# Turning the first two row tiles of a decoder block before their norm factor is known, and applying 1/rms to three half banks and to h later

## The chip, the cores and the metric

One core of a Trainium2 chip runs the whole kernel, float32 in and out. The metric is the device time of one execution in microseconds (us). Seven engines or queues matter: TensorE (PE, with PEld for its weight loads), VectorE (DVE), ScalarE (ACT), GpSimd (POOL) and the DMA queue that SyncE (SP) feeds.

## What is computed

A hybrid decoder block of 512 tokens and 1024 channels. The change touches only its first step, the RMS norm of the input and the first columns of the input projection:

```python
h = rmsnorm(x, norm1_g[l])            # x * 1/rms(token) * g(channel)
z = h @ w_in[l] + b_in[l]             # 1024 -> 6656 columns
z_glu, z_rx, z_rg, z_ga, z_gb = jnp.split(z, split_idx, axis=-1)
u = z_glu[..., :D_CONV] * jax.nn.sigmoid(z_glu[..., D_CONV:])
...
xb = causal_depthwise_conv(z_rx, lru_conv_w[l], lru_conv_b[l])
hb = rg_lru(xb, lru_wa[l], lru_ba[l], lru_wx[l], lru_bx[l], lru_lambda[l])
...
x = x + m @ w_mix_out[l]
h = rmsnorm(x, norm2_g[l])
x = x + (jax.nn.silu(h @ ffn_w1[l]) * (h @ ffn_w3[l])) @ ffn_w2[l]
return rmsnorm(x, norm_f_g)
```

Since 1/rms depends on the token alone, `(x * r) @ w` is also `(x @ w) * r`, token by token.

## The kernel before

**Split products.** Each factor of a product is held as two parts, a high part h (a cast to the fp32r type) and a low part l (the rest, `full - h`). A product is three matmuls per 128 channels: high weight by high input, high by low, low by high (`mm3`). An input projection tile is 128 output columns by 512 tokens, eight channel tiles c = 0 to 7, so 24 matmuls of 512 tokens, or twice 24 of 256 tokens when the two halves of the tokens are done apart.

**Weights** come as chunks of 512 KB, in a fixed list: SP loads a chunk into a raw buffer, ACT casts its high part (`L123`), POOL or DVE subtracts for the low part (`L119`). The first chunk (`in0`, columns 0 to 127) comes in two halves and goes through `first_parts` (L131): DVE casts the first half (`L133`), POOL casts the second and subtracts both. The second chunk (`in8`, columns 1024 to 1151, the gate of the same pair) is cast by ACT in two halves (`L138`, `L139`) and its low part is DVE's.

**The start** is the first block with a hand-written order on all engines (from L707). The four row tiles x0 to x3 hold 128 tokens each, with tokens on the partitions. For x0 and x1, DVE sums the squares of the second half of the channels (`half_sum`, L656), ACT those of the first half and then takes the root (`root`, L661 and L662), DVE takes the reciprocal, and DVE or ACT multiply the tile by it (`scale_half`, L672 and L670). Only then PE turns the tile, eight 128 by 128 transposes of it (`turn_rows`, L635), into banks tx of PSUM, 256 tokens of x0 and x1 next to each other. From these banks ACT writes the high part of the normed and weighted input for each channel tile (h10h to h17h, `turned_parts`, L644) and DVE the low part (h10l to h17l, L645). The name h13h is read as: first norm, channel tile 3, high part. Before any of that PE runs `WARM` matmuls on a tile of ones (L543).

PE then works through the half tiles in this order: `in0` for the first 256 tokens (`early_first`, L689, 24 matmuls in a hand-made order), `in8` for the first 256 (`early_mm(1, 0)`, L573), the turning of x2 and x3, `in1` for the first 256, `in0`, then the turning of the parameter rows (`L552`), `in8` and `in1` for the second 256, and `in9` for all 512 (`early_whole`). The banks are called z, with the column tile's number. x2 and x3 take the same road as x0 and x1 (half sum, root, reciprocal, scaling, turning), from data that are loaded behind the first two weight chunks.

**After that** a second hand-ordered block runs the other projection tiles, in which DVE's convolution steps are placed beside PE's tiles by a planner with fixed costs. `glu` joins banks z0 and z8 (a bias on ACT, a tanh on ACT, `u` on DVE at L915).

Of the kernel before, what the change touches and what calls it, by code (L numbers as in the profile page):

```python
# [33 lines left out]
HL = 5  # L34
AHEAD = 4
BEHIND = 5
WARM = 13

PACK = HB // 2
ROWS_G = HB + PACK  # L40
# [45 lines left out]
def tile_block(ctx, tc, a, out):  # L86
# [31 lines left out]
    def sub(eng, o, x, y):  # L118
        return eng.tensor_tensor(out=o, in0=x, in1=y, op=ALU.subtract)  # L119

    def split_to(h, l, full, eng, copy=act.copy):
# [6 lines left out]
        newest["sub" if eng is pool_e else "low"] = last.ins  # L128
        return h, l

    def first_parts(h, l, full):  # L131
        for cs in (slice(0, T), slice(T, 2 * T)):
            (pool_e if cs.start else vec).tensor_copy(h[:, cs], full[:, cs])  # L133
            newest["sub"] = sub(pool_e, l[:, cs], full[:, cs], h[:, cs].bitcast(F32)).ins
        return h, l

    def copy_halves(h, full):
        act.copy(h[:, :T], full[:, :T])  # L138
        act.copy(h[:, T:], full[:, T:])  # L139

    def lows_put_off(behind):
        while put_off:
# [55 lines left out]
    def emit_to(n):  # L198
        while emitted[0] < min(len(chunks), n):
            emit_chunk()  # L200
# [433 lines left out]
            at += P * (t % 2)  # L634
            pe.transpose(ps[b][:, at : at + P], xt[t][c // 4][:, (c % 4) * P : (c % 4 + 1) * P], ident)  # L635

    def turned_parts(hf, ps, some=range(ND)):
        cs = slice(hf * 256, hf * 256 + 256)
        for c in some:
            g = pc("norm1_g", c)  # L640
            b, at = spot(c, ps)
            p_ = ps[b][:, at : at + 256]
            h, l = (v[:, cs] for v in h1p[c])
            act.activation(h, p_, AF.Copy, scale=g)  # L644
            vec.scalar_tensor_tensor(out=l, in0=p_, scalar=g, in1=h.bitcast(F32), op0=ALU.mult, op1=ALU.subtract)  # L645

    def parts_of(pair_tiles, cs=slice(0, T)):
        return [(h[:, cs], l[:, cs]) for h, l in pair_tiles]
# [16 lines left out]
    def first_sums(t):  # L665
        return root(t, half_sum(t))
# [9 lines left out]
    EARLY_IN = [(GLU + j + 8 * o) for j in range(EARLY) for o in range(2)]  # L676
    early = []

    def early_first(between):
        m = EARLY_IN[0]  # L680
        early.append((m, w_tiles(f"in{m}", ND, 0), bank(f"z{m}")))
        _, ws, ps = early[0]
        order = [(0, 0), (0, 1), (1, 0), (0, 2), (1, 1), (0, 3), (1, 2), (2, 0), (2, 1), (2, 2), (0, 4), (2, 3), (1, 3), (0, 5)]
        order += [(1, 4), (0, 6), (1, 5), (2, 4), (0, 7), (2, 5), (2, 6), (1, 6), (2, 7), (1, 7)]
        xs = parts_of(h1p, HALVES[0])
        for n, (m, c) in enumerate(order):
            (wh, wl), (xh, xl) = ws[c], xs[c]
            l, r = ((wh, xh), (wh, xl), (wl, xh))[m]
            pe.matmul(ps[:, HALVES[0]], l, r, start=n == 0, stop=n == len(order) - 1)  # L689
            if n == 0:  # L690
                between()

    def early_mm(i, hf):
        m = EARLY_IN[i]
        if hf == 0:
            early.append((m, w_tiles(f"in{m}", ND, 0), bank(f"z{m}")))
        _, ws, ps = early[i]
        mm3(ps[:, HALVES[hf]], ws, parts_of(h1p, HALVES[hf]), lo_last=hf == 0)

    def early_whole(i):  # L700
        m = EARLY_IN[i]
# [5 lines left out]
    with tc.manual_schedule(engines={ET.PE, ET.Activation, ET.DVE, ET.SP, ET.Pool}):  # L707

        turned = [(bank if q < 5 else bank2)(f"tx0{q}") for q in range(6)]
        r0 = first_sums(0)  # L710
        vec.reciprocal(r0, r0)
        r1 = first_sums(1)
        scale_half(0, 0, r0)
        turn_rows(0, turned, 0)
        scale_half(0, 1, r0, True)
        rows_turned(0, n_first)
        vec.reciprocal(r1, r1)
        scale_half(1, 0, r1)
        turn_rows(1, turned, 0)
        emit_to(1)  # L720
        scale_half(1, 1, r1)
        turn_rows(0, turned, 1)
        load_chunk(1)
        load_x(2)
        load_x(3)
        load_chunk(2)
        load_chunk(3)
        turned_parts(0, turned, range(4))
        early_first(lambda: (turn_rows(1, turned, 1), turned_parts(0, turned, range(4, ND))))
        r2 = half_sum(2)  # L730
        emit_to(2)
        root(2, r2)
        early_mm(1, 0)
        vec.reciprocal(r2[1], r2[1])
        junk = [shortt(f"n1j3{h}") for h in range(2)]
        r3 = rstd_begin(xt[3][0], junk[0])
        for h in range(2):
            scale_half(2, h, r2[1])
        turned = [(bank2, bank)[q // 2](f"tx1{q}") for q in range(4)]
        turn_rows(2, turned)  # L740
        r3 = rstd_end(r3, xt[3][1], junk[1])
        for h in range(2):
            scale_half(3, h, r3)
        emit_to(3)
        load_head_rows()
        for i in range(len(parts)):
            if i not in first:
                load_rows(i)
        turn_rows(3, turned)
        emit_to(4)  # L750
        turned_parts(1, turned)
        early_mm(2, 0)
        early_mm(0, 1)
        rows_turned(n_first, n_rows)
        for m, n in ((GLU, 16), (GB, 8)):
            cols = par[:, col["b_in"] + m : col["b_in"] + m + n]
            act.activation(cols, cols, AF.Copy, scale=0.5)
        for i in (1, 2):
            early_mm(i, 1)
        early_whole(3)  # L760
    h1 = parts_of(h1p)

# [941 lines left out]
```

## Time and profile before

| what | value |
|---|---|
| three runs | 788.32, 788.86, 788.87 us; median 788.86 |
| the profiled execution's own time | 787.63 us |
| its span, first to last instruction | 785.9 us |
| PE busy | 777.6 us, 99% of the span |
| DVE, ACT, POOL busy | 86%, 60%, 46% |
| first projection matmul starts | 8.85 us into the span |
| `in9` starts (end of the start block's half tiles) | 29.34 us |

The page's chain that ended last follows work back from the last instruction: here it is PE nearly throughout. A row of the timeline gives the start, the duration, the engine, the line, the operation, what is written from what, and in brackets how long the engine had been idle and what released it. Durations overlap from one row to the next on the same engine, since an instruction begins before the one ahead of it has drained; the pitch from start to start is what a queue of them costs.

### The profile page before, as it was taken

The numbers are of one execution on the slowest core, as the hardware profiler recorded it, in microseconds if no ns is written. First come the engines' busy times: TensorE is split into PE (matmuls) and PEld (weight loads), VectorE is DVE, ScalarE is ACT, GpSimd is POOL, SyncE is SP. The second block draws the span as 40 slices with busy tenths as digits, with TensorE's granted clock in tenths as the row PEclk, the third lists the DMA queues.
The fourth block names the chain that finished last, engine by engine and source line by source line (L and its number), as shares of the span: only waits on it lengthen the run. The fifth ranks groups of instructions, "written<-read, shape, count | busy, mean of one in ns | idle before, by whom it ended". The sixth has DMA issues, their size and how long they took to land.

```text
span 785.9 us, 12508 instructions
## 1 busy us (share of the span) xinstructions
PE 777.6 (99%) x4328; PEld 680.0 (87%) x4328; DVE 677.2 (86%) x1074; ACT 473.8 (60%) x696; POOL 363.2 (46%) x353
## 2 busy tenths in 40 slices
PE   8999999999999999999999999999999999999996
PEld 8988888888888888888888898999999999888885
DVE  6389998889887987999799869897887897999956
ACT  7543678966785686564235676445545455656844
POOL 3367876799788989754530380121322322000000
PEclk9999999999999999999999999999999999999999
DMA  7656989899989868998978675688999998778652
GB/s 225 180 150 183 280 229 275 244 277 265 253 244 311 259 199 251 309 296 260 323 258 293 189 214 182 205 281 288 366 318 325 311 344 294 248 233 269 219 171 108
DMA packets 188561, 199.04 MB, mean 253 GB/s; under 512 B 15290, under 2 KB 149586, under 8 KB 188498
## 3 DMA queue, kind: packets, MB, share of 16 engines
q1 hardware_dynamic: 178066, 161.80, 68.2%
q0 software_dynamic: 10272, 36.18, 13.4%
q8 instruction: 34, 0.56, 0.3%
q14 instruction: 29, 0.24, 0.1%
q10 hardware_dynamic: 160, 0.27, 0.1%
HBM read 146.30 MB, written 38.80 MB: 236 GB/s over the span
## 4 chain that ended last, share of the span: by engine, by line
PE 99%; DVE 0%; issue 0%; ACT 0%
PE z L573 36%; PE fr L1429 25%; PE or L1195 13%; PE yb L573 7%; PE ya L573 6%; PE mxr L1195 5%; PE f L573 3%; PE g L1021 2%; PE fr L1475 1%; PE warm L543 1%; PE tx L635 0%; PE th L618 0%; PE z L689 0%; ACT of L1645 0%; PE orl L1195 0%
## 5 line engine op out<-in xcount | busy, mean ns | idle before, releaser
L821 DVE SCALAR_TENSOR_TENSOR cv<-u,par,cv 128x507 f32<-128x507 f32 (+15 forms) x240 | 162.2, 732 | 4.2 <-ACT cv L817 3.3
L119 POOL TENSOR_TENSOR hl_in<-raw_in,hl_in 128x1024 fp32r<-128x1024 f32 (+1 forms) x52 | 123.3, 2382 | 54.0 <-ACT hl_in L123 44.7
L119 POOL TENSOR_TENSOR fws<-fws 128x256 f32<-128x256 f32 x114 | 95.6, 840 | 40.1 <-DMA fws<-in_ffn_w_dram 34.6
L413 POOL DMA_DIRECT2D ot<-fwso x21 | 15.3, 730 | 148.9 <-DVE fwso L119 148.9
L1429 PE MATMUL fr<-hs_0h,hl_ft 128*128 128x256 f32 x320 | 59.2, 283 | 0.0
L123 ACT CAST hl_in<-raw_in 128x1024 fp32r<-128x1024 f32 x50 | 51.6, 1048 | 1.9 <-DMA raw_in<-in_w_in_dram 1.6
L1429 PEld LDWEIGHTS fr<-hs_0h,hl_ft 128*128 128x128 f32 x320 | 50.6, 192 | 0.0
L119 DVE TENSOR_TENSOR hl_ft<-raw_ft,hl_ft 128x1024 fp32r<-128x1024 f32 x39 | 47.5, 1218 | 2.8 <-ACT hl_ft L123 2.6
L123 ACT CAST hl_ft<-raw_ft 128x1024 fp32r<-128x1024 f32 x40 | 41.5, 1045 | 12.6 <-PE fr L1429 5.3
L123 ACT CAST hl_fb<-raw_fb 128x1024 fp32r<-128x1024 f32 x30 | 31.4, 1048 | 26.8 <-DMA raw_fb<-in_ffn_w_dram 20.2
L1429 PE MATMUL fr<-hs_0l,hl_ft 128*128 128x256 f32 x160 | 45.3, 283 | 0.0
L119 POOL TENSOR_TENSOR hl_ot<-raw_ot,hl_ot 128x1024 fp32r<-128x1024 f32 x1 | 2.4, 2412 | 84.9 <-ACT hl_ot L123 84.9
L119 DVE TENSOR_TENSOR hl_fb<-raw_fb,hl_fb 128x1024 fp32r<-128x1024 f32 x29 | 35.3, 1222 | 7.0 <-ACT hl_fb L123 7.0
L573 PE MATMUL z<-h10h,hl_in 128*128 128x512 f32 (+1 forms) x108 | 41.1, 382 | 0.0
L573 PE MATMUL z<-h12h,hl_in 128*128 128x512 f32 (+1 forms) x108 | 40.8, 379 | 0.0
L573 PE MATMUL z<-h14h,hl_in 128*128 128x512 f32 (+1 forms) x108 | 40.8, 379 | 0.0
L573 PE MATMUL z<-h15h,hl_in 128*128 128x512 f32 (+1 forms) x108 | 40.8, 379 | 0.0
L573 PE MATMUL z<-h16h,hl_in 128*128 128x512 f32 (+1 forms) x108 | 40.8, 379 | 0.0
L573 PE MATMUL z<-h13h,hl_in 128*128 128x512 f32 (+1 forms) x108 | 40.8, 379 | 0.0
L573 PE MATMUL z<-h11h,hl_in 128*128 128x512 f32 (+1 forms) x108 | 40.8, 379 | 0.0
L573 PE MATMUL z<-h17h,hl_in 128*128 128x512 f32 (+1 forms) x108 | 40.8, 379 | 0.0
L1441 ACT ACTIVATE c<-c 128x256 f32<-128x256 f32 x30 | 12.2, 416 | 40.4 <-DVE c L1144 40.4
(948 smaller groups left out, 2642.4 us busy)
## 6 DMA issues: line engine op xcount, KB each, us to landing
raw_in<-in_w_in_dram SPq DMA_DIRECT2D x51, 512.0 KB
fws<-in_ffn_w_dram SPq DMA_DIRECT2D x38, 512.0 KB
raw_ft<-fs SPq DMA_DIRECT2D x34, 512.0 KB
fs<-fws POOLq DMA_DIRECT2D x25, 512.0 KB, 5.1
fwso<-in_ffn_w_dram POOLq DMA_DIRECT2D x42, 256.0 KB, 7.6
ot<-fwso POOLq DMA_DIRECT2D x21, 512.0 KB, 6.2
raw_ob<-in_ffn_w_dram SPq DMA_DIRECT2D x33, 256.0 KB
raw_ot<-ot SPq DMA_DIRECT2D x33, 256.0 KB
```

Of the source, the lines that this page charges most:

```text
L119: return eng.tensor_tensor(out=o, in0=x, in1=y, op=ALU.subtract)
L123: copy(h, full)
L413: return queue.dma_start(dest, raw.rearrange("p (m n) -> p m n", n=256))
L543: pe.matmul(wp[:, :P], ones, ones, start=True, stop=True)
L573: pe.matmul(ps, l, r, start=i == 0, stop=i == n - 1)
L821: vec.scalar_tensor_tensor(out=acc[:, s:], in0=u[c][:, : T - s], scalar=dw(c, s), in1=acc[:, s:], op0=ALU.mult, op1=ALU.add)
L1021: pe.matmul(ps[:HB], head_chunk[0][:ROWS_G, g, h % 2, m, :], ext[h][m][:ROWS_G], start=m == 0, stop=m == 1)
L1195: pe.matmul(banks[i][:, cs], l_[:, ts], r_[:, cs], start=start and n == 0, stop=stop and n == 2, skip_group_check=again)
L1429: pe.matmul(ps[:, HALVES[i]], lw[:, c, :], rx_, start=not (again or i or c or m), stop=bool(i and c == 3 and m == 2), skip_group_check=True,)
L1441: act.activation(c[:, LO], c[:, LO], AF.Silu)
L1475: pe.matmul(self.r4[:, HALVES[i]], lw, rx_, start=not (i or c or m), stop=bool(i and c == 3 and m == 2), skip_group_check=True)
```

## The change

x0 and x1 are turned as they arrive, without the multiplication by 1/rms. The eight transposes of x0 stand together, then the turn of the weights g, then the eight of x1. `WARM` falls from 13 to 8. The four scalings of x0 and x1 go, and ACT's root of x1 moves behind the second chunk's cast.

What follows from them is unscaled: h10 to h17 for the first 256 tokens, and so the first halves of the banks z0, z8 and z1. Later, DVE spreads the two columns of 1/rms over a 128 by 256 tile (`rspread`), PE turns it in two transposes (`rp`), ACT copies it to SBUF (`by`), and DVE multiplies the three half banks by it (`early_scaled`). For the column tiles that come after, the first 256 tokens of h are made anew for each channel tile: DVE adds high and low (`norm_sum`), multiplies by `by` (`norm_scale`), ACT casts the new high part, and DVE (even c) or POOL (odd c) subtracts for the new low part (`norm_low`).

`in0`'s second half is cast by DVE instead of POOL, one step inside the row of low parts (`between`); `in8`'s second half by POOL instead of ACT; `in8`'s low part on DVE now stands ahead of x2's half sum instead of behind it; the chunk of the fifth column tile is split earlier (`emit_to(5)`).

```diff
--- before.py
+++ after.py
@@ -34,7 +34,7 @@
 HL = 5
 AHEAD = 4
 BEHIND = 5
-WARM = 13
+WARM = 8
 
 PACK = HB // 2
 ROWS_G = HB + PACK
@@ -128,15 +128,23 @@
         newest["sub" if eng is pool_e else "low"] = last.ins
         return h, l
 
+    first_steps = []
+
     def first_parts(h, l, full):
-        for cs in (slice(0, T), slice(T, 2 * T)):
-            (pool_e if cs.start else vec).tensor_copy(h[:, cs], full[:, cs])
+
+        def cast(cs):
+            vec.tensor_copy(h[:, cs], full[:, cs])
+
+        def low(cs):
             newest["sub"] = sub(pool_e, l[:, cs], full[:, cs], h[:, cs].bitcast(F32)).ins
+
+        for f in (cast, low):
+            first_steps.append([lambda f=f, cs=cs: f(cs) for cs in (slice(0, T), slice(T, 2 * T))])
         return h, l
 
     def copy_halves(h, full):
         act.copy(h[:, :T], full[:, :T])
-        act.copy(h[:, T:], full[:, T:])
+        pool_e.tensor_copy(h[:, T:], full[:, T:])
 
     def lows_put_off(behind):
         while put_off:
@@ -634,7 +642,7 @@
             at += P * (t % 2)
             pe.transpose(ps[b][:, at : at + P], xt[t][c // 4][:, (c % 4) * P : (c % 4 + 1) * P], ident)
 
-    def turned_parts(hf, ps, some=range(ND)):
+    def turned_parts(hf, ps, some=range(ND), between={}):
         cs = slice(hf * 256, hf * 256 + 256)
         for c in some:
             g = pc("norm1_g", c)
@@ -643,6 +651,22 @@
             h, l = (v[:, cs] for v in h1p[c])
             act.activation(h, p_, AF.Copy, scale=g)
             vec.scalar_tensor_tensor(out=l, in0=p_, scalar=g, in1=h.bitcast(F32), op0=ALU.mult, op1=ALU.subtract)
+            for f in between.get(c, ()):
+                f()
+
+    def norm_sum(c):
+        h, l = (v[:, HALVES[0]].bitcast(F32) for v in h1p[c])
+        hn = shortt(f"hn{c}")[:, HALVES[0]]
+        vec.tensor_tensor(out=hn, in0=h, in1=l, op=ALU.add)
+        return hn
+
+    def norm_scale(c, hn, by):
+        vec.tensor_tensor(out=hn, in0=hn, in1=by, op=ALU.mult)
+        act.copy(h1p[c][0][:, HALVES[0]], hn)
+
+    def norm_low(c, hn):
+        h, l = (v[:, HALVES[0]] for v in h1p[c])
+        sub(pool_e if c % 2 else vec, l, hn, h.bitcast(F32))
 
     def parts_of(pair_tiles, cs=slice(0, T)):
         return [(h[:, cs], l[:, cs]) for h, l in pair_tiles]
@@ -676,19 +700,17 @@
     EARLY_IN = [(GLU + j + 8 * o) for j in range(EARLY) for o in range(2)]
     early = []
 
-    def early_first(between):
+    def early_first():
         m = EARLY_IN[0]
         early.append((m, w_tiles(f"in{m}", ND, 0), bank(f"z{m}")))
         _, ws, ps = early[0]
-        order = [(0, 0), (0, 1), (1, 0), (0, 2), (1, 1), (0, 3), (1, 2), (2, 0), (2, 1), (2, 2), (0, 4), (2, 3), (1, 3), (0, 5)]
-        order += [(1, 4), (0, 6), (1, 5), (2, 4), (0, 7), (2, 5), (2, 6), (1, 6), (2, 7), (1, 7)]
+        order = [(0, 0), (0, 1), (0, 2), (1, 0), (0, 3), (1, 1), (0, 4), (0, 5), (2, 0), (1, 2), (2, 1), (0, 6), (2, 2), (1, 3)]
+        order += [(0, 7), (2, 3), (1, 4), (1, 5), (2, 4), (2, 5), (1, 6), (2, 6), (2, 7), (1, 7)]
         xs = parts_of(h1p, HALVES[0])
         for n, (m, c) in enumerate(order):
             (wh, wl), (xh, xl) = ws[c], xs[c]
             l, r = ((wh, xh), (wh, xl), (wl, xh))[m]
             pe.matmul(ps[:, HALVES[0]], l, r, start=n == 0, stop=n == len(order) - 1)
-            if n == 0:
-                between()
 
     def early_mm(i, hf):
         m = EARLY_IN[i]
@@ -697,6 +719,10 @@
         _, ws, ps = early[i]
         mm3(ps[:, HALVES[hf]], ws, parts_of(h1p, HALVES[hf]), lo_last=hf == 0)
 
+    def early_scaled(i, by):
+        z = early[i][2][:, HALVES[0]]
+        vec.tensor_tensor(out=z, in0=z, in1=by, op=ALU.mult)
+
     def early_whole(i):
         m = EARLY_IN[i]
         early.append((m, w_tiles(f"in{m}", ND, 0), bank(f"z{m}")))
@@ -709,29 +735,27 @@
         turned = [(bank if q < 5 else bank2)(f"tx0{q}") for q in range(6)]
         r0 = first_sums(0)
         vec.reciprocal(r0, r0)
-        r1 = first_sums(1)
-        scale_half(0, 0, r0)
-        turn_rows(0, turned, 0)
-        scale_half(0, 1, r0, True)
+        turn_rows(0, turned)
         rows_turned(0, n_first)
-        vec.reciprocal(r1, r1)
-        scale_half(1, 0, r1)
-        turn_rows(1, turned, 0)
+        s1 = half_sum(1)
+        turn_rows(1, turned)
         emit_to(1)
-        scale_half(1, 1, r1)
-        turn_rows(0, turned, 1)
+        casts, lows = first_steps
+        casts[0]()
+        lows[0]()
         load_chunk(1)
         load_x(2)
         load_x(3)
         load_chunk(2)
         load_chunk(3)
-        turned_parts(0, turned, range(4))
-        early_first(lambda: (turn_rows(1, turned, 1), turned_parts(0, turned, range(4, ND))))
+        turned_parts(0, turned, between={0: (casts[1], lows[1])})
+        early_first()
+        emit_to(2)
+        r1 = root(1, s1)
         r2 = half_sum(2)
-        emit_to(2)
         root(2, r2)
+        vec.reciprocal(r2[1], r2[1])
         early_mm(1, 0)
-        vec.reciprocal(r2[1], r2[1])
         junk = [shortt(f"n1j3{h}") for h in range(2)]
         r3 = rstd_begin(xt[3][0], junk[0])
         for h in range(2):
@@ -741,22 +765,49 @@
         r3 = rstd_end(r3, xt[3][1], junk[1])
         for h in range(2):
             scale_half(3, h, r3)
-        emit_to(3)
+        vec.reciprocal(r1, r1)
+        spread = longt("rspread")
+        for t, r in enumerate((r0, r1)):
+            vec.tensor_scalar(out=spread[:, t * P : (t + 1) * P], in0=ones, scalar1=r, scalar2=None, op0=ALU.mult)
         load_head_rows()
         for i in range(len(parts)):
             if i not in first:
                 load_rows(i)
+        emit_to(3)
         turn_rows(3, turned)
-        emit_to(4)
+        rp = bank("rp")
+        for t in range(2):
+            pe.transpose(rp[:, t * P : (t + 1) * P], spread[:, t * P : (t + 1) * P], ident)
         turned_parts(1, turned)
         early_mm(2, 0)
+        by = longt("by")[:, HALVES[0]]
+        act.copy(by, rp[:, HALVES[0]])
+        emit_to(4)
         early_mm(0, 1)
+        hn = {}
+
+        def to_norm(c0, c1):
+            for c in range(c0, c1 + (c1 == ND)):
+                if c < ND:
+                    hn[c] = norm_sum(c)
+                    norm_scale(c, hn[c], by)
+                if c:
+                    norm_low(c - 1, hn[c - 1])
+
+        to_norm(0, 3)
+        emit_to(5)
+        early_scaled(0, by)
+        early_mm(1, 1)
+        to_norm(3, 4)
         rows_turned(n_first, n_rows)
         for m, n in ((GLU, 16), (GB, 8)):
             cols = par[:, col["b_in"] + m : col["b_in"] + m + n]
             act.activation(cols, cols, AF.Copy, scale=0.5)
-        for i in (1, 2):
-            early_mm(i, 1)
+        to_norm(4, 6)
+        early_scaled(1, by)
+        to_norm(6, 8)
+        early_mm(2, 1)
+        early_scaled(2, by)
         early_whole(3)
     h1 = parts_of(h1p)
```

On PE the opening reads like this before. The names: tx are the turned banks, x_122 and x_123 the row tiles x0 and x1, par_ps the weights g, z_239 the bank of `in0`, hl_in its weights.

```order
L543 MATMUL warm<-ones 128x128 x13
L635 MATMUL tx_177<-ident,x_122 128x128 x2
...
L552 MATMUL par_ps_200<-ident,rows_115 128x8
L635 MATMUL tx_177<-ident,x_123 128x128 x2
...
L635 MATMUL tx_180<-ident,x_122 128x128 x2
...
L689 MATMUL z_239<-h10h,hl_in_212 128x256
L635 MATMUL tx_180<-ident,x_123 128x128 x2
...
L689 MATMUL z_239<-h11h,hl_in_212 128x256
L689 MATMUL z_239<-h10l,hl_in_212 128x256
```

And like this with the change (transposes of the other banks left out in both):

```order
L551 MATMUL warm<-ones 128x128 x8
L643 MATMUL tx_172<-ident,x_122 128x128 x2
...
L643 MATMUL tx_175<-ident,x_122 128x128 x2
...
L560 MATMUL par_ps_192<-ident,rows_115 128x8
L643 MATMUL tx_172<-ident,x_123 128x128 x2
...
L643 MATMUL tx_175<-ident,x_123 128x128 x2
...
L713 MATMUL z_238<-h10h,hl_in_208 128x256
L713 MATMUL z_238<-h11h,hl_in_208 128x256
L713 MATMUL z_238<-h12h,hl_in_208 128x256
L713 MATMUL z_238<-h10l,hl_in_208 128x256
```

All sixteen transposes now stand ahead of the first projection matmul, and the first three high parts are used before the first low part.

On DVE, from the last low part of the first 256 tokens to the scaling of x3, before (n1j is the half sum's throwaway output, hl_in_278 the second chunk, x_124 to x_126 the tiles x2 and x3):

```order
L645 SCALAR_TENSOR_TENSOR h17l<-tx_180,par,h17h 128x256
L656 ISA n1j_276,stats<-x_124 128x512
L656 ISA stats 128x1
L119 TENSOR_TENSOR hl_in_278<-raw_in_222,hl_in_278 128x1024
L734 RECIPROCAL stats<-stats 128x1
L585 TENSOR_SCALAR stats<-stats 128x1
L672 TENSOR_SCALAR x_124<-x_124,stats 128x512 x2
```

With the change:

```order
L653 SCALAR_TENSOR_TENSOR h17l<-tx_175,par,h17h 128x256
L119 TENSOR_TENSOR hl_in_263<-raw_in_211,hl_in_263 128x1024
L680 ISA n1j_270,stats<-x_124 128x512
L680 ISA stats 128x1
L757 RECIPROCAL stats<-stats 128x1
L593 TENSOR_SCALAR stats<-stats 128x1
L696 TENSOR_SCALAR x_124<-x_124,stats 128x512 x2
```

The half sum of x2, on which its root, reciprocal and scaling wait, has moved behind the subtraction for the second chunk.

On DVE behind the copy of the parameters, before:

```order
L645 SCALAR_TENSOR_TENSOR h17l<-tx_320,par,h17h 128x256
L556 COPY par<-par_ps_428 128x400
L915 SCALAR_TENSOR_TENSOR u_520<-sg_518,z_239 128x512
```

With the change (hn is the full value of one channel tile, by the turned 1/rms, z_276 the bank of `in8`, sg the tanh for the first `u`):

```order
L564 COPY par<-par_ps_476 128x400
L660 TENSOR_TENSOR hn_486<-h14h,h14l 128x256
L664 TENSOR_TENSOR hn_486<-hn_486,by 128x256
L660 TENSOR_TENSOR hn_491<-h15h,h15l 128x256
L664 TENSOR_TENSOR hn_491<-hn_491,by 128x256
L119 TENSOR_TENSOR h14l<-hn_486,h14h 128x256
L724 TENSOR_TENSOR z_276<-z_276,by 128x256
L660 TENSOR_TENSOR hn_497<-h16h,h16l 128x256
L664 TENSOR_TENSOR hn_497<-hn_497,by 128x256
...
L966 SCALAR_TENSOR_TENSOR u_567<-sg_565,z_238 128x512
L119 TENSOR_TENSOR h16l<-hn_497,h16h 128x256
```

Between the copy and `u` stand the new steps of the channel tiles 4 to 7 and the scaling of the second bank; eleven more of them stand ahead of the copy. PE's row has one trace of this: in the bank of `in9` the matmuls of the channel tiles 6 and 7 come later, with six matmuls of the next column tile set in between.

## The prediction

> **What bounds the kernel now.** I read the page's totals and chain first, then the chain in order of time, then the first 40 us engine by engine, since the change ends there.
>
> ```profile
> span 785.9 us, 12508 instructions
> PE 777.6 (99%) x4328; PEld 680.0 (87%) x4328; DVE 677.2 (86%) x1074; ACT 473.8 (60%) x696; POOL 363.2 (46%) x353
> PE 99%; DVE 0%; issue 0%; ACT 0%
> ```
>
> The chain is TensorE's queue itself. In order of time (start, length, what):
>
> ```profile
> 1.08 4.83 PE warm L543 x26
> 5.91 1.17 issue
> 7.08 0.63 PE tx L635 x4
> ...
> 9.68 2.94 PE z L689 x23
> ...
> 17.25 5.75 PE z L573 x48
> ...
> 23.56 49.49 PE z L573 x240
> ```
>
> PE stands still before 7.08 us and has a few short gaps until 9.68; from there it is full. So the change is worth what it moves the end of the start block, and whatever PE gains or loses there arrives unchanged at the end. Two pitches follow: 48 matmuls of 256 tokens in 5.75 us are 0.12 us each; of the 240, 48 are of that kind (5.76 us) and 192 of 512 tokens, so (49.49 - 5.76) / 192 = 0.228 us each.
>
> What held the start back is in these rows of the timeline:
>
> ```profile
> 4.51 0.63 ACT L661 ACTIVATE n1j<-x 128x512 f32<-128x512 f32 x1 [1.48 <-DMA x<-in_x_dram]
> 5.87 0.63 ACT L661 ACTIVATE n1j<-x 128x512 f32<-128x512 f32 x1 [0.27 <-DMA x<-in_x_dram]
> 7.59 0.42 DVE L133 CAST hl_in<-raw_in 128x512 fp32r<-128x512 f32 x1
> 7.79 1.09 PE L635 MATMUL tx<-ident,x 128*128 128x128 f32 x8
> 8.32 0.47 ACT L644 ACTIVATE h10h<-tx,par 128x256 fp32r<-128x256 f32 x1 [0.26 <-PE tx L635]
> 8.85 0.39 PE L689 MATMUL z<-h10h,hl_in 128*128 128x256 f32 x1
> 9.23 0.48 DVE L645 SCALAR_TENSOR_TENSOR h11l<-tx,par,h11h 128x256 fp32r<-128x256 f32 x1
> 10.41 0.48 DVE L645 SCALAR_TENSOR_TENSOR h14l<-tx,par,h14h 128x256 fp32r<-128x256 f32 x1
> 10.92 0.47 ACT L644 ACTIVATE h17h<-tx,par 128x256 fp32r<-128x256 f32 x1
> 11.58 0.48 DVE L645 SCALAR_TENSOR_TENSOR h17l<-tx,par,h17h 128x256 fp32r<-128x256 f32 x1
> ```
>
> x0 is there at 4.51, x1 at 5.87. From then to the turn of x1 (7.79) go root, reciprocal and scaling. The low parts come at (11.58 - 9.23) / 6 = 0.39 us each, and h17h begins only at 10.92, when h14l (10.41 + 0.48), which reads the same bank, is done.
>
> **The change, term by term.** *First bank.* x1 can be turned from 5.9 instead of 7.79. Before, h10h began 0.53 us behind that turn; now at 6.4, ending at 6.9. The weights are then the later side: `in0` follows x1 in the queue.
>
> ```profile
> 5.90:7.10 1.20, 0.03 (x2) 0.05 (x1) 1.18 (x4) 1.13 (x4) 0.00 (x0) 1.00 1.16 324
> 8.85:12.46 3.61, 3.61 (x30) 3.59 (x29) 3.61 (x9) 3.61 (x10) 2.55 (x3) 1.00 1.06 351
> ```
>
> The last column of such a row of a stretch is the GB/s moved. Half a chunk (262 KB) at 324 GB/s takes 0.81 us, so the halves of `in0` are there at about 6.7 and 7.5. DVE casts the first (0.42) to 7.1, and PE begins at 7.15, 1.7 us earlier. But DVE also casts the second, in the middle of its low parts: 7.6 to 8.0. So h11l begins at 8.0, h14l at 9.2, h17h (behind h14l) at 9.7, done at 10.15, h17l at 10.35. In PE's new order nine matmuls follow the one that reads h17h: 10.2 + 10 x 0.12 = 11.4 for the first matmul of `in8`, against 12.46 (x2's turn began at 15.34, in a row below, and `in8` takes 24 x 0.12 = 2.88 before it). Gain so far 1.06 us. The eight transposes of x0 (1.09) fall into the wait for x1. `in8` itself is ready: ACT casts its first half behind h17h, in half of the 1.09 that a whole cast takes below, to 10.7; POOL subtracts `in0`'s halves first (1.2 each by its row below) and is done with its half of `in8` at 10.8 if a cast costs it no more than a subtraction, while PE asks for it at the ninth matmul, 12.4.
>
> *x2 and x3.* This is where I expect most of the loss.
>
> ```profile
> 11.97 0.68 DVE L656 CUSTOM_DVE_ANT_0 n1j<-x 128x512 f32<-128x512 f32 x1
> 12.58 1.22 DVE L119 TENSOR_TENSOR hl_in<-raw_in,hl_in 128x1024 fp32r<-128x1024 f32 x1
> 13.07 0.29 ACT L662 ACTIVATE stats<-stats 128x1 f32<-128x1 f32 x1
> 14.09 0.88 DVE L672 TENSOR_SCALAR x<-x,stats 128x512 f32<-128x512 f32 x2
> 15.16 0.88 DVE L672 TENSOR_SCALAR x<-x,stats 128x512 f32<-128x512 f32 x2
> 15.34 1.91 PE L635 MATMUL tx<-ident,x 128*128 128x128 f32 x16
> 17.00 0.36 PE L573 MATMUL z<-h10h,hl_in 128*128 128x256 f32 x1
> 29.34 0.40 PE L573 MATMUL z<-h10h,hl_in 128*128 128x512 f32 x1
> ```
>
> DVE's subtraction for `in8` (1.22, pitch 1.14) now stands before the half sum of x2: 10.75 to 11.95, then the half sum at 11.9, as late as before (11.97). ACT's root of x2 waits for it: 12.7 instead of 13.07, so 0.37 earlier, and ACT's squares of x3, its root and the scalings keep that distance: the last scaling ends at 16.04 - 0.37 = 15.67. PE is through with `in8` at 11.4 + 2.88 = 14.3, finds x2 scaled at 14.1 to 14.6, and must wait for x3. Sixteen transposes took 15.34 to 17.00, 0.104 each. The last four of x3, and the two new ones for 1/rms, follow the scaling: 15.7 + 6 x 0.104 = 16.35 for the first matmul of `in1`, against 17.00. The two new transposes cost 0.21 in this. The spreads wait for no one new: the reciprocal of x1 and two spreads of 128 columns follow x3's scaling on DVE. No row shows them; they cost between nothing and 0.44 each (half of the pair of 128x512 above). By the columns a spread is a quarter of that, 0.11; the three then end within the 0.42 of x3's last four transposes. At the upper end they add 0.9. **Net 0.65 us earlier.**
>
> *From there to `in9`.* The queue of PE is the same 96 matmuls and the rows' turn in another order, so `in9` comes at 29.34 - 0.65 = 28.7, if nothing is late. `in1`'s low part is the nearest:
>
> ```profile
> 14.83 2.18 ACT L123 CAST hl_in<-raw_in 128x1024 fp32r<-128x1024 f32 x2
> 15.95 4.76 POOL L119 TENSOR_TENSOR hl_in<-raw_in,hl_in 128x1024 fp32r<-128x1024 f32 x2 [4.47 <-ACT hl_in L123]
> ```
>
> The cast moves to 14.5, POOL's subtraction to 15.6, ending 2.4 later at 18.0; PE needs it 16 matmuls behind 16.35, at 18.3. It fits by 0.3.
>
> *The new work for h.* Before `in9`, 23 new steps of 256 tokens stand on DVE, eight casts on ACT, four subtractions on POOL. The nearest rows for them, and for what stands between:
>
> ```profile
> L119 DVE TENSOR_TENSOR fwso<-fwso 128x256 f32<-128x256 f32 x63 | 26.3, 419 | 11.2 <-DMA fwso<-in_ffn_w_dram 10.8
> L1144 DVE TENSOR_TENSOR mxs<-mxv 128x256 f32<-128x256 f32 x4 | 2.2, 550 | 0.0
> L123 ACT CAST os1p<-os 128x256 fp32r<-128x256 f32 x11 | 4.4, 401 | 0.7 <-DVE os L1144 0.7
> L119 POOL TENSOR_TENSOR fws<-fws 128x256 f32<-128x256 f32 x114 | 95.6, 840 | 40.1 <-DMA fws<-in_ffn_w_dram 34.6
> 23.59 0.57 DVE L556 COPY par<-par_ps 128x400 f32<-128x400 f32 x1 [2.91 <-PE par_ps L555]
> 25.21 1.28 ACT L941 ACT_TABLE_LOAD   x1
> 26.66 0.69 ACT L941 ACTIVATE sg<-z,par 128x512 f32<-128x512 f32 x1 [0.17 <-PE z L573]
> ```
>
> 23 x 0.42 = 9.7 us of DVE lie under PE, which is why I cost them at nothing; without the cover that is their price. The tight place is behind the copy of the parameters: it waits for PE's turn of the rows, which moves behind `in8`'s second half: 23.59 + 2.88 - 0.65 = 25.8, done at 26.4. Six steps (sum and product of tiles 4 and 5, low part of 4, product of bank z8) at 0.42 end at 28.9; then ACT's table load and tanh, 30.9; then h16h, 31.3. PE reads h16h as the 16th matmul behind 28.7 (three of them already of the next tile): 28.7 + 15 x 0.228 = 32.1. Spare 0.8 us. h17h is done at 31.7, POOL's h17l (0.84) at 32.6; PE reads it five matmuls later, at 33.5: spare 0.9. h16l stands on DVE behind `u` (0.7, from 30.9) and ends at 32.0, needed at 33.0. With the slow row (550) the six steps cost 0.8 more and the spare is used up exactly; were they as slow as POOL's 840, PE would stand 1.7 us. I take 419, of 63 instances. Behind `in9` the order on every engine is that of before.
>
> **The sum**: 785.9 - 0.65 = 785.2 us of span. The profiled execution's own time, 787.63, is 1.2 under the median of the three runs, 788.86, so I give the difference, not the level, to the median: **788.2 us**, 0.08% faster. A difference under 0.2% (1.6 us) is what a measurement of this kernel can hardly tell from none.
>
> **Rivals.** *The x2 chain does not bind* (14%): if x3 is scaled by 15.3, PE keeps the 1.06 and pays only 0.21 for two transposes: 788.0. For it: only the half sum's place holds it back. Against it: the working above has PE waiting some 0.15 to 0.4 us for x3. *The x2 chain does not move at all* (16%): no row shows when x3 lands; if it lands just as ACT took it before, the scaling ends at 16.04, `in1` starts at 16.66 and 0.3 us stay: 788.5. Against it: `in0`, `in8`, x2 and x3 are 4 x 524 KB behind x1, and at 324 to 351 GB/s there at 11.8 to 12.3, while ACT asks for x3 behind the root at 12.7. *The new work for h is late* (12%): place, point and price above; the end is 0.65 - (excess over 0.8): 788.3 to 789.9.
>
> *TensorE's half pace lasts longer: slower* (6%). These stretches show the pace (PE's instructions in brackets):
>
> ```profile
> 1.08:4.50 3.42, 3.42 (x16) 3.42 (x17) 0.00 (x0) 1.67 (x3) 0.29 (x1) 1.00 0.74 264
> 4.50:5.90 1.40, 1.40 (x12) 1.22 (x11) 0.89 (x4) 1.04 (x4) 0.00 (x0) 1.00 1.02 335
> ```
>
> Sixteen passes of 128 columns took 3.42 us, 0.214 each, and the next ones 0.117, although the granted clock reads 1.00 in both. Thirteen warming matmuls are 26 passes; eight are 16, ending at 1.08 + 3.42 = 4.50, just as x0 comes. Then PE works with gaps: x0's turn to 5.4 or so, a wait for x1 to 5.9, its turn to 6.8, a wait to 7.15, then matmuls with stalls to 10.2. If the full pace needs PE to be busy without a break and comes only behind `in8`, 48 matmuls run 0.094 to 0.12 us longer each, 4.5 to 5.8 us, of which about 1 goes into waits that are there anyhow: some 3.5 us worse than forecast, 791.7. It decides once `in0`'s and `in8`'s matmuls are slow for more than about 24 of them. Against it: before, PE idled 1.17 us at 5.91 and the pace stayed, and no new gap is as long.
>
> [...]
>
> **How the numbers follow.** Forecast 49%, the rivals 14, 16, 12 and 6%, and 3% for a gain over 1.6 us by something that I don't see. The first four lie within 0.2% but for a late tail of the new work (2%); the half pace adds 6% on the slow side. So faster 3%, same 89%, slower 8%. The range 787.3 to 789.7 takes in the gain of 1.06, the new work late by 1.5 and the spread of the three runs (0.55) at either end; the clock's case lies outside.
>
> **What would show it.** PE's first projection matmul at 7.1 to 7.3; `in8`'s first at 11.3 to 11.6; x2's half sum near 11.9 and a short wait of PE within the turn of x3; `in1` at 16.2 to 16.6; `in9` at 28.5 to 28.9, and no idle time of PE within it. Wrong would be: `in1` at or behind 17.0; matmuls of 256 tokens at a pitch over 0.2 before 15 us; PE waiting for a cast of h16h or POOL's h17l near 32 us; or a difference that arises behind 40 us, where the order is as before.

## The result and the profile after

The changed kernel takes 792.11 us (median of six runs, 791.17 to 794.01) against 788.87 for the kernel before (six runs, 787.41 to 790.17): a ratio of 1.0048, 95% interval 1.0032 to 1.0065. It is slower by 0.48%; the forecast was 788.2 us and no difference that can be measured. The profiled execution took 792.57 us.

The page of the changed kernel, first lines:

```profile
span 790.8 us, 12531 instructions
PE 780.6 (99%) x4320; PEld 680.1 (86%) x4320; DVE 693.4 (88%) x1097; ACT 475.6 (60%) x703; POOL 369.0 (47%) x357
```

DVE has 16.2 us more to do than before (677.2). PE's share hides the loss. The two rows below, one from each kernel's chain in order of time (start, length, what; the kernel before first), give the start of the same stage far behind the change:

```profile
311.53 20.43 PE yb L573 x90
```

```profile
315.20 20.43 PE yb L581 x90
```

PE is 3.67 us late there, and the medians differ by 3.24. Behind that point the two profiled executions differ by another 1.2 us of span: from 520 to 635 us the chain of the changed kernel runs over loads and DVE, that of the kernel before over PE alone. One profile of each can't tell whether the change has a part in that; the runs of the kernel before alone spread over 2.8 us. So the 3.67 us are to be found, and the timeline of PE has them before 40 us:

```profile
1.09 3.78 PE L551 MATMUL warm<-ones 128*128 128x128 f32 x16 [1.09 <-DVE ones L544]
4.66 1.91 PE L643 MATMUL tx<-ident,x 128*128 128x128 f32 x8
...
6.71 1.32 PE L643 MATMUL tx<-ident,x 128*128 128x128 f32 x8
8.00 0.38 PE L713 MATMUL z<-h10h,hl_in 128*128 128x256 f32 x1
...
12.22 0.28 PE L581 MATMUL z<-h10h,hl_in 128*128 128x256 f32 x1
...
15.11 2.01 PE L643 MATMUL tx<-ident,x 128*128 128x128 f32 x16
18.75 0.52 PE L780 MATMUL rp<-ident,rspread 128*128 128x128 f32 x2 [1.63 <-DVE rspread L771]
19.03 0.36 PE L581 MATMUL z<-h10h,hl_in 128*128 128x256 f32 x1
...
31.37 0.40 PE L581 MATMUL z<-h10h,hl_in 128*128 128x512 f32 x1
...
33.59 0.50 PE L581 MATMUL z<-h14l,hl_in 128*128 128x512 f32 x1
...
34.51 0.50 PE L581 MATMUL z<-h15l,hl_in 128*128 128x512 f32 x1 [0.18 <-POOL h15l L119]
...
36.28 0.50 PE L581 MATMUL z<-h16h,hl_in 128*128 128x512 f32 x1 [0.58 <-ACT h16h L665]
```

`in8` begins at 12.22, a little ahead of the 12.46 before. PE then stands for the spread of 1/rms (`rp` waits 1.63 us), and `in1` begins at 19.03 instead of 17.00: 2.03 us lost. `in9` keeps that (31.37 against 29.34), and within it PE waits for new parts of h. From `in9` to the steady stage another 3.67 - 2.03 = 1.64 us go, though the two bracketed waits make only 0.76. In pitches from start to start, of which 0.23 is the plain one, h14l comes 0.38 us behind its forerunner, h15l 0.58 and h16h 0.97, and the matmul behind each of them 0.33 or 0.34: together about 1.56 us over the plain pitch.

What PE waits for is DVE. Its timeline, the new steps and a few around them:

```profile
16.36 2.54 DVE L771 TENSOR_SCALAR rspread<-ones,stats 128x128 f32<-128x128 f32 x2
18.82 0.47 DVE L653 SCALAR_TENSOR_TENSOR h10l<-tx,par,h10h 128x256 fp32r<-128x256 f32 x1
...
22.46 2.48 DVE L664 TENSOR_TENSOR hn<-hn,by 128x256 f32<-128x256 f32 x1
24.86 0.41 DVE L660 TENSOR_TENSOR hn<-h11h,h11l 128x256 f32<-128x256 f32 x1
25.31 0.42 DVE L664 TENSOR_TENSOR hn<-hn,by 128x256 f32<-128x256 f32 x1
...
29.19 2.33 DVE L660 TENSOR_TENSOR hn<-h14h,h14l 128x256 f32<-128x256 f32 x1
31.56 0.85 DVE L664 TENSOR_TENSOR hn<-hn,by 128x256 f32<-128x256 f32 x1
...
33.79 0.94 DVE L660 TENSOR_TENSOR hn<-h16h,h16l 128x256 f32<-128x256 f32 x1
```

The same operation on the same shape takes 0.41 us or 2.48. GpSimd's timeline beside it:

```profile
16.27 2.35 POOL L119 TENSOR_TENSOR hl_in<-raw_in,hl_in 128x1024 fp32r<-128x1024 f32 x1 [5.56 <-DMA rows<-in_conv_b_out_dram]
22.26 2.40 POOL L119 TENSOR_TENSOR hl_in<-raw_in,hl_in 128x1024 fp32r<-128x1024 f32 x1 [3.64 <-ACT hl_in L123]
...
28.85 2.40 POOL L119 TENSOR_TENSOR hl_in<-raw_in,hl_in 128x1024 fp32r<-128x1024 f32 x1 [1.80 <-ACT hl_in L123]
31.20 0.92 POOL L119 TENSOR_TENSOR h13l<-hn,h13h 128x256 fp32r<-128x256 f32 x1
33.72 0.73 POOL L119 TENSOR_TENSOR h15l<-hn,h15h 128x256 fp32r<-128x256 f32 x1 [1.59 <-ACT h15h L665]
```

Every long DVE step of this stretch begins while a GpSimd subtraction runs, and ends about 0.3 us behind it: 22.46 + 2.48 = 24.94 against 22.26 + 2.40 = 24.66; 33.79 + 0.94 = 34.73 against 33.72 + 0.73 = 34.45. The low parts of L653, which read PSUM, aren't touched (0.47 or 0.48 in all places).

**The theory**: a DVE step that reads two operands from SBUF, or copies from SBUF to SBUF, stands still until the running GpSimd subtraction is done. The rivals: the half pace of TensorE at the start (which I had priced at 791.7), and new DVE steps that are slow, or too many, by themselves.

### The profile page after: what moved, and what is told of

Read it like the earlier page. It is cut to its first block, busy times and chain, and to the rows that moved or that the text cites. A ratio compares the mean times of both kernels' runs of the same rounds, so it can differ in the third digit from the quotient of the medians.

```text
span 790.8 us, 12531 instructions
## 1 busy us (share of the span) xinstructions
PE 780.6 (99%) x4320; PEld 680.1 (86%) x4320; DVE 693.4 (88%) x1097; ACT 475.6 (60%) x703; POOL 369.0 (47%) x357
## 4 chain that ended last, share of the span: by engine, by line
PE 81%; DVE 8%; DMA 6%; issue 2%; ACT 1%; POOL 1%; DVEq 0%; ACTq 0%
PE z L581 33%; PE or L1246 13%; PE fr L1480 10%; PE yb L581 7%; PE ya L581 6%; PE mxr L1246 5%; DMA fwso<-in_ffn_w_dram 3%; PE f L581 3%; DMA raw_fb<-in_ffn_w_dram 2%; PE g L1072 2%; PE fr L1526 1%; DMA fws<-in_ffn_w_dram 1%; DVE hl_fb L119 1%; DVE fwso L119 1%; DVE hl_ft L119 1%
## 5 line engine op out<-in xcount | busy, mean ns | idle before, releaser
L119 POOL TENSOR_TENSOR fws<-fws 128x256 f32<-128x256 f32 x114 | 97.2, 854 | 39.4 <-DMA fws<-in_ffn_w_dram 33.9
L123 ACT CAST hl_ft<-raw_ft 128x1024 fp32r<-128x1024 f32 x40 | 41.3, 1045 | 12.1 <-PE fr L1480 7.4
```

Of the source, the lines that this page charges most:

```text
L123: copy(h, full)
```

## The experiments

All starts are from one profiled execution each; the ratios are against runs of the kernel before on the same chip. The column lnmp is the start of that row in the chain, two matmuls ahead of yb, as a measure of where PE stands when the start is over; the others are starts on PE's timeline, all in us.

| kernel | `in8` | `in1` | `in9` | lnmp | median us | ratio, 95% interval |
|---|---|---|---|---|---|---|
| before | 12.46 | 17.00 | 29.34 | 311.06 | 788.2 to 788.9 | |
| changed | 12.22 | 19.03 | 31.37 | 314.74 | 792.11 | 1.0048, 1.0032 to 1.0065 |
| e1: 13 warming matmuls | 12.62 | 19.43 | 31.77 | 315.14 | 793.02 | 1.0057, 1.0042 to 1.0072 |
| e2: spread on ACT | 12.27 | 17.14 | 29.48 | 314.00 | 791.12 | 1.0038, 1.0025 to 1.0052 |
| e3: GpSimd kept out | 12.26 | 17.13 | 29.47 | 313.45 | 790.83 | 1.0030, 1.0017 to 1.0043 |
| e6: other order | 12.29 | 17.17 | 29.52 | 311.69 | 789.02 | 1.0005, 0.9993 to 1.0018 |
| e9: low parts of `in0` swapped | 14.04 | 19.43 | 31.77 | 315.77 | 794.47 | one run |
| e8: e6 with two edits at the start | 14.59 | 19.35 | 31.69 | 313.86 | 791.03 | 1.0028, 1.0015 to 1.0041 |
| e10: e8 with PE's order made to fit | 11.92 | 16.68 | 29.02 | 311.18 | 788.81 | 1.0009, 0.9996 to 1.0021 |

**The disputed cost by itself (e5).** Four steps that feed nothing, in the kernel before, beside a pair of GpSimd subtractions:

```diff
+        spare = early[0][2][:, HALVES[1]]
+        vec.tensor_scalar(out=spare[:, :P], in0=ones, scalar1=2.0, scalar2=None, op0=ALU.mult)
+        vec.tensor_scalar(out=pr[0][:, :P], in0=ones, scalar1=2.0, scalar2=None, op0=ALU.mult)
+        vec.tensor_tensor(out=pr[0][:, P : 2 * P], in0=ones, in1=spare[:, :P], op=ALU.mult)
+        vec.tensor_tensor(out=pr[1][:, :P], in0=ones, in1=ident, op=ALU.mult)
```

> The kernel before with four added DVE steps of 128x128 behind x3's scaling, beside POOL's subtractions from 15.95 to 20.7 us; they feed nothing. A: scalar product from SBUF to PSUM; B: scalar product from SBUF to SBUF; C: product of an SBUF and a PSUM operand; D: product of two SBUF operands. [...] Rival 1 (every DVE access to SBUF waits for GpSimd): all four are held. Rival 2 (DVE merely shares bandwidth): B and D take at most twice A and C.

DVE's timeline (`spare`, in bank z, is PSUM; `ones`, `ident` and probe are SBUF), then GpSimd's:

```profile
15.96 0.29 DVE L746 TENSOR_SCALAR z<-ones 128x128 f32<-128x128 f32 x1
16.15 2.27 DVE L747 TENSOR_SCALAR probe<-ones 128x128 f32<-128x128 f32 x1
18.34 0.27 DVE L748 TENSOR_TENSOR probe<-ones,z 128x128 f32<-128x128 f32 x1
18.54 2.30 DVE L749 TENSOR_TENSOR probe<-ones,ident 128x128 f32<-128x128 f32 x1
```

```profile
15.95 4.74 POOL L119 TENSOR_TENSOR hl_in<-raw_in,hl_in 128x1024 fp32r<-128x1024 f32 x2 [4.45 <-ACT hl_in L123]
```

The four rows say which steps wait, and they are those of the theory above: A and C, with PSUM on one side, take 0.29 and 0.27; B (SBUF to SBUF) and D (two SBUF inputs) take 2.27 and 2.30, until the first and the second subtraction end (about 18.3 and 20.7). Nothing connects these steps to GpSimd's data. Both rivals of the expectation fall: neither do all accesses wait, nor is it a sharing at half rate. The one run took 790.96 us, since the low parts behind these steps come late (h10l begins at 20.76 instead of 17.46, and PE waits 1.02 us for it).

**Warming undone (e1).**

```diff
-WARM = 8
+WARM = 13
```

> The changed kernel with 13 warming matmuls again in place of 8; nothing else. Theory (DVE steps that read two operands from SBUF, or copy from SBUF to SBUF, stand still as long as a GpSimd subtraction runs): the loss is made between 16 and 31 us, so the end stays at 791.5 to 792.5; the spread still takes over 2 us and the products of the norm beside POOL's subtractions about 2.5. Rival (TensorE's half pace at the start is the cause): the first projection matmul comes back to about 7.2, in1 to about 16.4, and the time falls to 790 or less.

`in1` at 19.43, 793.02 us, and DVE's rows for the spread and the first product are 2.54 and 2.48 as in the changed kernel, although x0's turn now runs at full pace (1.04 us). The loss isn't the clock's at the start. It came out 0.5 above the upper end expected, with `in8` 0.4 us later, since PE is through with the warming only at 6.4.

**The spread on ACT (e2).**

```diff
-            vec.tensor_scalar(out=spread[:, t * P : (t + 1) * P], in0=ones, scalar1=r, scalar2=None, op0=ALU.mult)
...
         emit_to(3)
+            act.activation(spread[:, t * P : (t + 1) * P], ones, AF.Copy, scale=r)
```

> The changed kernel with the two spreads of 1/rms made by ACT (a copy with a scale) instead of DVE; nothing else. Theory (DVE waits for the running GpSimd subtraction): in1 starts at about 17.1 instead of 19.03, the first product of the norm is still held by POOL's subtraction for in9, and the end comes at 790.2 to 791.2. Rival (what is late at 16 us is x3's scaling or the turn, whoever makes the spread): in1 stays at 18.5 or later and the time at 792.

`in1` at 17.14: the spread alone cost 19.03 - 17.14 = 1.89 us, and the median is at the upper end expected (791.12). lnmp has come back by only 0.74, because the wait went on: the sum of channel tile 1 now meets GpSimd's subtraction for `in9` (the first product, which I expected to be held, had just passed), and PE waits 1.11 us for h16h. The rows of DVE and PE:

```profile
21.39 2.62 DVE L660 TENSOR_TENSOR hn<-h11h,h11l 128x256 f32<-128x256 f32 x1
```

```profile
35.34 0.50 PE L581 MATMUL z<-h16h,hl_in 128*128 128x512 f32 x1 [1.11 <-ACT h16h L665]
```

**GpSimd kept out (e3).** DVE subtracts for `in1` and `in9` too, `in16` is split later.

```diff
-        wchunk(f"in{m}", w_in[:, :, m * P : (m + 1) * P], ND, P, lo=vec if len(chunks) == 1 else pool_e)
+        wchunk(f"in{m}", w_in[:, :, m * P : (m + 1) * P], ND, P, lo=vec if len(chunks) in (1, 2, 3) else pool_e)
...
-        emit_to(5)
```

> The changed kernel with GpSimd kept out of the stretch from 15 to 31 us: the low parts of in8, in1 and in9 are subtracted by DVE, and in16 is split only behind in9's matmuls, as in the kernel before. Theory (DVE waits for the running GpSimd subtraction): the spreads take 0.15 to 0.25 us each, all sums and products of the norm about 0.42, in1 starts at about 17.0, in9 at about 29.4 with a stall of some 0.6 at h16h, and the time is 789 to 790, although DVE has three subtractions of 1.2 us more to do. Rival (the new steps are slow by themselves, or DVE has too many of them): sums and products stay at 0.9 to 2.5 us and the time is 792 or more.

The two spreads take 0.46 together, the sums and products 0.41 to 0.43 except three beside GpSimd's short low parts (0.85 to 0.95). So the steps aren't slow by themselves. But the time is 790.83, above the 789 to 790 expected. PE's rows say where the rest is:

```profile
32.77 0.50 PE L581 MATMUL z<-h16h,hl_in 128*128 128x512 f32 x1 [0.40 <-ACT h16h L665]
33.54 0.51 PE L581 MATMUL z<-h16l,hl_in 128*128 128x512 f32 x1 [0.27 <-DVE h16l L119]
...
37.48 0.50 PE L581 MATMUL z<-h10h,hl_in 128*128 128x512 f32 x1 [0.54 <-POOL hl_in L119]
```

DVE now has two subtractions of 1.22 us more ahead of the steps for h (not three, as I had written: that for `in8` was DVE's already), and `in16`, which is split too late, costs the last wait. I had sized h16h and left `in16` out.

**The same GpSimd work in another order (e6).** The casts of `in1` and `in9` go ahead of the turned parts, so that GpSimd's two subtractions run while DVE makes low parts from PSUM; the spread is on ACT; `in16` comes behind the steps for h, its low part on DVE.

```diff
         emit_to(3)
+            act.activation(spread[:, t * P : (t + 1) * P], ones, AF.Copy, scale=r)
+        emit_to(4)
         turn_rows(3, turned)
...
-        emit_to(4)
...
-        emit_to(5)
...
         to_norm(6, 8)
+        emit_to(5)
```

> The changed kernel in another order, with the same GpSimd work for in1 and in9: the spreads on ACT, the casts of in1 and in9 ahead of the turned parts of the second half (as in the kernel before), so that GpSimd subtracts while DVE makes low parts that read PSUM, and in16 split behind the steps for h, its low part by DVE. Theory (only steps with both operands in SBUF wait for GpSimd): in1 at about 17.1, the norm's sums and products about 0.42 each but for those beside GpSimd's four short low parts, in9 at about 29.4, no wait for h16h, 788.7 to 789.5. Rival (DVE has too much work, whatever GpSimd does): waits for h16h of 0.5 us or more stay and the time is 790 or more.

GpSimd's and then DVE's timeline:

```profile
16.34 4.77 POOL L119 TENSOR_TENSOR hl_in<-raw_in,hl_in 128x1024 fp32r<-128x1024 f32 x2 [5.56 <-ACT hl_in L123]
```

```profile
18.20 0.49 DVE L653 SCALAR_TENSOR_TENSOR h10l<-tx,par,h10h 128x256 fp32r<-128x256 f32 x1 [1.76 <-ACT h10h L652]
...
20.95 0.48 DVE L653 SCALAR_TENSOR_TENSOR h17l<-tx,par,h17h 128x256 fp32r<-128x256 f32 x1
21.34 0.42 DVE L660 TENSOR_TENSOR hn<-h10h,h10l 128x256 f32<-128x256 f32 x1
21.86 0.43 DVE L664 TENSOR_TENSOR hn<-hn,by 128x256 f32<-128x256 f32 x1
```

From 16.34 to 21.11 GpSimd subtracts and DVE's eight low parts keep their 0.39 pitch; the first sum begins when GpSimd is done, and takes 0.42. From `in9` to 40 us PE loses only 0.4 us, at h16l and h17l. 789.02, within the range expected, ratio 1.0005 (0.9993 to 1.0018): with another order and two small moves 0.63 of the 3.68 us at lnmp are left, and the times can't be told from those of the kernel before.

**The start (e9, e8, e10).** In e2, e3 and e6 `in8` begins at 12.26 to 12.29 and not at the 11.4 of the forecast. DVE's rows of e3, and GpSimd's:

```profile
7.79 1.04 DVE L136 CAST hl_in<-raw_in 128x512 fp32r<-128x512 f32 x1 [0.21 <-DMA raw_in<-in_w_in_dram]
8.75 0.47 DVE L653 SCALAR_TENSOR_TENSOR h11l<-tx,par,h11h 128x256 fp32r<-128x256 f32 x1
```

```profile
7.27 1.28 POOL L119 TENSOR_TENSOR hl_in<-raw_in,hl_in 128x512 fp32r<-128x512 f32 x1 [5.83 <-DVE hl_in L136]
```

It is the same wait: the cast of `in0`'s second half stands until GpSimd's first subtraction ends (at 8.55; the cast ends at 8.83). e9 swaps GpSimd's two low parts, so that none runs beside this cast:

```diff
-        lows[0]()
...
-        turned_parts(0, turned, between={0: (casts[1], lows[1])})
+        turned_parts(0, turned, between={0: (casts[1], lows[1], lows[0])})
```

> The changed kernel with GpSimd's two low parts of in0 issued in the other order (the second half's first), so that no GpSimd subtraction runs while DVE casts that second half; nothing else. Theory (DVE's copies from SBUF to SBUF wait for the running GpSimd subtraction, and this ate most of the first gain): that cast takes 0.42 instead of 1.04 us where x0's turn was at full pace, h11l starts at about 8.1 instead of 8.75, and in8's first matmul at about 11.4 instead of 12.26; the end is still near 791 to 792, since the waits of 16 to 31 us stay. Rival (x1 or the weights land too late for the predicted gain): in8 stays at 12.2.

The cast took 0.43 and h11l began at 8.43, but `in8` came at 14.04, and 794.47 us: a miss. PE's order for `in0` still asks for the first half's low weights early, and they now come last; PE stood 1.52 us for them and then fell to half pace (matmuls of 256 tokens 0.21 us apart instead of 0.12). e8 has the same swap, x2's half sum ahead of `in8`'s low part, and the order of e6:

```diff
+        r2 = half_sum(2)
         emit_to(2)
         r1 = root(1, s1)
-        r2 = half_sum(2)
```

> The order of the run with the casts ahead (spread on ACT, in1 and in9 cast early, in16 late and on DVE), and two edits at the start: GpSimd's low parts of in0 in the other order, and x2's half sum ahead of in8's low part on DVE. Theory: in8's first matmul at 11.4, x3 scaled by about 15.5, in1 at about 16.3, in9 at about 28.7, which are the values that the prediction had; 787.8 to 788.6, under the kernel before by 0.2 to 0.8. Rival (another bound, such as x3's landing or ACT's root, holds in1 at 17): 788.7 to 789.5, as the run with the order alone.

The same miss: 791.03. Its stretches (the last columns are the granted clock, the share of the DMA engines and GB/s):

```profile
7.41:11.17 3.76, 1.80 (x8) 1.17 (x8) 3.31 (x9) 2.88 (x8) 2.55 (x3) 0.97 1.07 346
11.17:14.32 3.15, 3.15 (x14) 3.15 (x15) 2.93 (x8) 3.05 (x11) 0.50 (x1) 0.50 1.15 307
```

In the first PE was busy 1.80 of 3.76 us, with a wait of 1.57 at its end; in the second the granted clock is 0.50 and a matmul of 256 tokens takes 0.21 instead of 0.12. e10 lets PE's order follow the swap, low weights of the second half first and none early:

```diff
-        order = [(0, 0), (0, 1), (0, 2), (1, 0), (0, 3), (1, 1), (0, 4), (0, 5), (2, 0), (1, 2), (2, 1), (0, 6), (2, 2), (1, 3)]
-        order += [(0, 7), (2, 3), (1, 4), (1, 5), (2, 4), (2, 5), (1, 6), (2, 6), (2, 7), (1, 7)]
+        order = [(0, 0), (0, 1), (0, 2), (1, 0), (0, 3), (0, 4), (1, 1), (0, 5), (0, 6), (1, 2), (1, 3), (2, 4), (2, 5), (1, 4)]
+        order += [(2, 6), (1, 5), (0, 7), (2, 7), (1, 6), (2, 0), (2, 1), (2, 2), (1, 7), (2, 3)]
```

> The run with the order and the two edits at the start, and TensorE's order for in0 made to fit: the matmuls with low weights of the second half first, since GpSimd now makes these first, and none of them early, so that TensorE has no long gap between 7 and 12 us. Theory (the gap of 1.57 us at in0's low part put TensorE to half pace until 14.3, and that is all that was lost there): matmuls of 256 tokens at 0.12 us throughout, in8's first at about 11.8, in1 at about 16.4, in9 at about 28.8; 787.6 to 788.4, level with the kernel before or under it by up to 0.1%. Rival (the start has another bound): in1 at 17.0 or later and 788.8 or more.

PE's timeline of e10:

```profile
7.62 0.36 PE L713 MATMUL z<-h10h,hl_in 128*128 128x256 f32 x1 [0.53 <-DVE hl_in L136]
...
11.92 0.28 PE L581 MATMUL z<-h10h,hl_in 128*128 128x256 f32 x1
...
16.68 0.36 PE L581 MATMUL z<-h10h,hl_in 128*128 128x256 f32 x1
...
29.02 0.40 PE L581 MATMUL z<-h10h,hl_in 128*128 128x512 f32 x1
```

`in1` is 0.32 us ahead of the kernel before, and so is `in9`. At lnmp it is 0.12 behind: h16l and h17l still come late by 0.4 us together. The profiled execution took 787.76; the median of twelve, 788.81, is above the 787.6 to 788.4 expected, and the ratio 1.0009 (0.9996 to 1.0021) tells no difference from the kernel before. No version was found that beats it.

## Why the prediction was wrong

**The step that failed** is the price of the new DVE work, in two places. "They cost between nothing and 0.44 each ... By the columns a spread is a quarter of that, 0.11" was the term for the spreads; measured, the pair took 2.54 us and cost `in1` 1.89 (e2); with no GpSimd step beside it, the pair takes 0.46 (e3). "23 x 0.42 = 9.7 us of DVE lie under PE, which is why I cost them at nothing" was the term for h; measured, the eight products took 6.3 us instead of 3.4, two sums 2.33 and 0.94 instead of 0.42 each, the spare of 0.8 was gone, and 1.64 us went between `in9` and the steady stage. Both prices came from rows that have no GpSimd subtraction beside them, and the working put GpSimd's subtractions on the same microseconds (15.6 to 18.0 for `in1`) without asking what they do to DVE.

The trace of before had the sign, in the row that I took as "the slow row (550)". Its tile view gives the least, middle and greatest duration in ns, and the timeline the first instance and GpSimd's work beside it:

```profile
L1144 DVE TENSOR_TENSOR mxs<-mxv x4: 412/418/952, 393.4 to 419.0; 128x256 f32<-128x256 f32 x4
```

```profile
393.41 0.95 DVE L1144 TENSOR_TENSOR mxs<-mxv 128x256 f32<-128x256 f32 x1
```

```profile
391.29 2.79 POOL L119 TENSOR_TENSOR fws<-fws 128x256 f32<-128x256 f32 x2 [2.75 <-DMA fws<-in_ffn_w_dram]
```

550 was a mean of three at 0.42 and one at 0.95, and this one ended at 394.36, 0.28 us behind GpSimd's 394.08. That is the wait of e5, in the kernel before.

**The first gain** was mis-sized: 0.24 us at `in8` instead of 1.06. That h17h, behind h14l, sets it was right. But h11l began at 8.71 instead of 8.0 and h14l at 9.89 instead of 9.2. In the profiled execution of the changed kernel this was the half pace: x0's turn took 1.91 us and x1's 1.32 (e10: 1.25 and 1.09), so the turned rows came late. In e2 and e3, where they came earlier (h10l at 7.39 and 7.10 instead of 7.98), it was the cast held by GpSimd; h11l begins at 8.7 or 8.8 in all three. So x2's half sum stood at 12.62 instead of 11.9, and x3 was scaled at 16.37 instead of 15.67: x2's chain did not move forward, as the rival with 16% had it, but because DVE's half sum was late and not a load; the wait for the spread hid that. In e10, with both out of the way (and x2's half sum ahead of `in8`'s low part), the gain at `in8` is 0.54 and at `in1` 0.32, half of the 0.65 forecast. What is missing there stands in DVE's row of e10: the cast waits for the load of the second half until 8.13, which the working had landed at about 7.5, and h11l begins at 8.47.

```profile
8.13 0.43 DVE L136 CAST hl_in<-raw_in 128x512 fp32r<-128x512 f32 x1 [0.27 <-DMA raw_in<-in_w_in_dram]
```

Two slips of the working changed nothing: 15.7 + 6 x 0.104 is 16.32 and not 16.35, and h17l is read six matmuls behind h16h, as its 33.5 has it, and not five.

**The rivals.** Half pace (791.7 us) had nearly the right number for the wrong reason: the matmuls of `in8` run at 0.12 in the changed kernel, and e1 keeps the loss. Its 791.7 was worked out from an assumption of mine, that the full pace needs PE to be busy without a break, which no run shows; in e8 and e9 half pace came behind waits of 1.57 and 1.52 us. That PE would wait for h16h (12%, up to 789.9) named the right place, with the price of one mechanism missing. That all behind `in9` is as before was right as far as the start of yb: from 40 us to there both kernels differ by a constant.

## What to carry to other kernels

Before a step is priced at "hidden on DVE", note for each operand whether it lies in SBUF or PSUM, and what GpSimd runs at that time: here a step with two SBUF inputs, or a copy or scalar product from SBUF to SBUF, cost the rest of the running GpSimd subtraction (2.30 and 2.27 us in e5, against 0.27 and 0.29 with PSUM on one side), and the whole queue behind it paid. Put GpSimd's long steps beside DVE steps that read PSUM, or give the small ones to ACT; here such an order, with the spread on ACT and one subtraction on DVE, was worth 3.1 us (792.11 to 789.02; 1.0048 to 1.0005 against the kernel before). And where a group's mean lies off that of its neighbours, look at its least and greatest before using it as a bound.

## What the runs showed of the hardware that was not expected

- In e5 the wait lasted until the running subtraction was done: a 128x128 product of two SBUF operands took 2.30 us beside a 128x1024 GpSimd subtraction (2.37 us, half of the pair's 4.74). DVE did get in between two such subtractions that stand back to back (B ended at 18.42, D began at 18.54 and waited anew, until 20.84, with the pair ending at 20.69).
- It was not only beside subtractions that DVE was late: in e8 and e10 x2's half sum, which reads x2 twice, took 1.02 and 1.05 us instead of 0.68 beside a GpSimd cast of 0.61 and 0.60.
- GpSimd was late in its turn. In the changed kernel two of its 128x256 subtractions, 0.74 us each at the median in the kernel before, took 5.07 us while DVE ran steps back to back, 0.59 to 0.74 us from start to start and most of them with two SBUF inputs:

```profile
356.70 5.07 POOL L119 TENSOR_TENSOR fws<-fws 128x256 f32<-128x256 f32 x2 [3.70 <-DMA fws<-in_ffn_w_dram]
```

- Half pace came behind waits of PE of about 1.5 us: in e8, behind one of 1.57, the granted clock was 0.50 from 11.17 to 14.32; in e9, behind one of 1.52, the matmuls went from 0.12 to 0.21 us from start to start at about 12.1, 0.9 us behind the end of the wait, and kept that until 15.32 (granted clock 0.66 on the mean from 11.16 to 14.00). From `in0`'s first matmul to the end of the wait PE was busy 48% of the time in e8 (1.80 of 3.76 us), and 52% in e9 (1.77 of 3.38, without the wait's last 0.06). Behind a gap of 1.17 us in the kernel before there was no half pace: the eight transposes from 7.79 took 1.09 us.
- At the very start the column of the granted clock reads 1.00 while the passes take 0.21 us each, and the end of that pace differs from one execution to the next (x0's turn took 1.91 us in the changed kernel's, 1.06 in e3's). There the pitch of the rows has to be read, not the column.
